# The input projections in another order, and all sixteen gates computed within dilated attention

## The chip, the cores and the metric

The kernel runs on one core of a Trainium2 chip. The metric is the device time of one execution in microseconds (us); less is better. TensorE multiplies matrices, VectorE (DVE), ScalarE (ACT) and GpSimd (POOL) work on the elements, and transfers are issued from the queues of SyncE (SP) and of ScalarE.

## The reference

One decoder layer for 1024 tokens of width 1024, in float32. One input projection gives eight parts; two head groups read them, each group has a SiLU gate, and the result goes through an output projection, a residual and a layer norm:

```python
h = x @ w_in
c_q, c_kv, k_rope, g_a, q_b, k_b, v_b, g_b = jnp.split(h, offs, axis=-1)
y_a = mla_attention(c_q, c_kv, k_rope, ...) * jax.nn.silu(g_a)   # 8 heads, causal
y_b = dilated_attention(q_b, k_b, v_b) * jax.nn.silu(g_b)        # 8 heads, dilations 1, 4, 16
x = layernorm(DEEPNORM_ALPHA * x + jnp.concatenate([y_a, y_b], -1) @ w_out, ln_g, ln_b)
```

The latents c_q (384 columns) and c_kv (256) pass an RMS norm and an up-projection before the latent attention; the dilated queries and keys are rotated.

## The kernel before

Every float32 operand of a projection is split into a high and a low part, and each product is made of three matmuls (`PASSES`: high by high, high by low, low by high) that accumulate in one bank of PSUM. The high part is an ACT copy, the low part a subtraction on DVE, or on POOL for weights (`hi_lo`, L77; `wload`, L110). The 1024 rows of the contraction are eight tiles, `KD`; the tokens are two halves `s` of 512 or eight blocks `i` of 128.

The projections follow each other in this order: the first four tiles of the latents while x arrives, with the contraction outermost and all eight banks in use (L127 to L153); the up-projections' weights are loaded, scaled and stored as float16 pairs beside them (`u_load`, `u_scales`, `u_split`, L208 to L212); the fifth latent tile (L269); the dilated values, block by block (`v_block`), with the latents' normalisation between them (`rms_apply`, L243); half of the latent attention's values (`va_block`, L347); the dilated queries (`qk_block(0, ...)`); the other half of the latent values; the keys (`qk_block(1, ...)`); and then eight of the sixteen gates, which are those of the first half of the tokens (`gate_now`, L451, called in L455 and L507).

Queries, keys and values are brought to float16 pairs by a power of two. The largest value over all partitions takes a way through DRAM and back (`pow2`, L289): a DVE reduction, a store, a load that spreads it, and another DVE reduction that waits for that load. Only then do `q_split`, `k_split` and `v_split` write the pairs to DRAM (`q_d`, `k_d`, `v_d`), from which `load_qk` (L478) brings them back by transposing transfers, two for the queries and two for the keys of each pair of heads.

Dilated attention has 32 steps (four pairs of heads, two halves, four blocks). A step is scores (`dil_scores`, TensorE), the mask and the row's least value (L551, DVE), the exponential (`dil_expo`, ACT), the split of the probabilities (`dil_high`, `dil_low`), a transposing transfer for every two steps (`ptd`), and the product with the values five steps later (`dil_values`). The mask is loaded whole (`mraw`, L498) and brought to the scores' units by two DVE instructions (L501, L502). Between the steps `next(fill, None)` emits a piece of other work for TensorE: half a gate (12 matmuls), and after the last gate a piece of what the latent attention needs first (`latents_first`, L678). The list `FILL` (L800) names the steps that have one piece; the eight gates of the second half of the tokens are 16 such pieces, and step 22 has the last of them. Those gates use Tanh from the table that Exp is in, and one DVE instruction more than the eight before, which use Silu; each weight of a gate is loaded twice in the program, once for each half of the tokens.

The memory of a phase lies where that of an earlier one was: `gy`, `b4` (nine slots of 4 KB), `b8` and the mask `mp` of dilated attention take the place of the projections' weights (`wp`) and working tiles (`st`), and a tile waits for what lay in its place. x lies on the other side, its first half so that it can be given up early (`stX0`). Each engine executes its instructions in the order in which a planner put them: it goes by the order of the program, and by the times that it reckons with where an instruction isn't ready.

The latent attention and the output projection follow. The second key tile of the latent attention (`kB`, L845) lies in `b8`; beside the last pair of heads the first weights and gated rows of the output projection are prepared in the memory of the latents (`open_pools(stO, side="right")`, L910; `load_wo`, `load_y`).

Of the kernel before, what the change touches and what calls it, by code (L numbers as in the profile page):

```python
# [19 lines left out]
P = 128  # L20
# [20 lines left out]
def tile_hybrid_layer(ctx, tc, xT, xres, w_c, w_c2, w_vr, w_k, w_q, w_g, w_u, w_o,  # L41
# [53 lines left out]
    stG, stX0, st1, stPS1 = (ctx.enter_context(ExitStack()) for _ in range(4))  # L95
# [5 lines left out]
    wp, st = l1("wp", 10), l1("st")  # L101
# [8 lines left out]
    def wload(src, n, name, pool=None):  # L110
        r = rtile(name + "r")
# [5 lines left out]
    xs = [[xp[s].tile([P, 2, 512], F32R, name=f"x{k}{s}") for s in range(2)] for k in range(KD)]  # L117
    acc = [bank(f"acc{m}") for m in range(8)]
# [3 lines left out]
    SMALL = {2: ((qg_s, qg), (kvg_s, kvg)), 4: ((csd, cs_dil), (csp, cs_pe), (mmla, msk_mla))}  # L122
    heat = st.tile([P, 512], F16, name="heat")
    nc.vector.memset(heat, 0.0)
    for _ in range(HEAT):
        nc.tensor.matmul(acc[7], heat[:, :P], heat, start=True, stop=True)
    for k in range(KD):  # L127
        if k in SMALL:  # what is needed later only does not hold the first rows up
            for d, src in SMALL[k]:
                tc.keep_in_program_order(nc.scalar.dma_start(d, src))  # L130
        xr = [rtile(f"xr{k}{s}")[:, :512] for s in range(2)]
        if k == 0:  # the first product waits for little
            r = rtile("wc0r")
            ws = wp.tile([P, 2, 544], F32R, name="wc0", tag="w")
            for c in (slice(0, P), slice(P, 512)):
                sync.dma_start(r[:, c], w_c[0, :, c])
                nc.scalar.copy(ws[:, 0, c], r[:, c])
                if c.start == 0:
                    sync.dma_start(xr[0], xT[:P, half(0)])
                    nc.vector.tensor_copy(xs[0][0][:, 0], xr[0])  # L140
                    nc.vector.tensor_sub(xs[0][0][:, 1], xr[0], xs[0][0][:, 0].bitcast(F32))
# [6 lines left out]
        order = [(s, m, pz) for s in range(2) for m in range(4) for pz in PASSES]  # L148
        if k == 0:
            order = [(s, m, pz) for s in range(2) for pz in PASSES for m in range(4)]  # L150
# [60 lines left out]
    for a in uraw:  # L211
        u_split(*a)  # L212
# [912 lines left out]
```

## Time and profile before

| | us |
|---|---|
| median of three runs | 660.19 |
| lowest and highest run | 656.34, 662.71 |
| the profiled execution, its span from the first to the last instruction | 659.7 |
| TensorE busy in that span | 601.3 |
| VectorE busy | 417.7 |
| ScalarE busy | 327.5 |
| GpSimd busy | 317.8 |

No time other than its span is given for the profiled execution. Busy TensorE includes matmuls that overlap in the pipeline, so that a stretch in which it is always busy can still hold fewer or more matmuls; the number of matmuls in a stretch tells how fast it went.

### The profile page before, as it was taken

What the parts mean: (1) busy time and instruction counts of PE and PEld (TensorE: products, weight loads), DVE (VectorE), ACT (ScalarE), POOL (GpSimd) and SP (SyncE); (2) the same over time, 40 slices, a digit from 0 to 9 for tenths busy, and PEclk for the clock granted to TensorE, in tenths of its full rate; (3) what the DMA queues carried; (4) which work ended last, traced back from release to release, by engine and by line L of the source; (5) the groups of instructions that cost most, each with busy time, mean ns of one, the idle gap of its engine ahead of it and who ended that gap; (6) DMA issues with size and microseconds to landing.
All of it is one profiled execution on the core that took longest, in us unless ns stands there. A gap on an engine that the chain in (4) does not pass through costs nothing.

```text
span 659.7 us, 11049 instructions
## 1 busy us (share of the span) xinstructions
PE 601.3 (91%) x3975; PEld 439.9 (67%) x3975; DVE 417.7 (63%) x865; ACT 327.5 (50%) x661; POOL 317.8 (48%) x338
## 2 busy tenths in 40 slices
PE   8999999999999979399999987889789878799995
PEld 5777999788688858166666644545445445678884
DVE  5671299443234042357876798598699998454886
ACT  3467323334423254168675785488588876440000
POOL 2148323925814265267774576374357595640000
PEclk9999999999999979689999978898799997999998
DMA  8695112876812469999999799939869999861051
GB/s 287 203 285 171 33 33 80 116 226 158 222 43 94 36 240 177 182 219 230 230 209 195 160 302 201 199 58 195 154 116 181 156 224 242 200 202 67 1 192 64
DMA packets 200854, 108.53 MB, mean 165 GB/s; under 512 B 158688, under 2 KB 176608, under 8 KB 200672
## 3 DMA queue, kind: packets, MB, share of 16 engines
q1 hardware_dynamic: 194608, 96.36, 63.5%
q10 hardware_dynamic: 6192, 11.47, 7.7%
q8 instruction: 31, 0.51, 0.4%
q14 instruction: 23, 0.19, 0.1%
HBM read 48.30 MB, written 20.71 MB: 105 GB/s over the span
## 4 chain that ended last, share of the span: by engine, by line
PE 36%; DMA 28%; DVE 15%; POOL 6%; issue 6%; ACT 5%; SPq 3%; ACTq 0%; DVEq 0%; POOLq 0%
PE op L880 8%; DMA pT<-ph 6%; DMA ptd<-p 5%; PE gP L429 5%; DMA kk<-k_d 3%; PE op L1009 3%; DMA xr<-in_xT_dram 3%; PE Od L623 3%; PE vbA L223 3%; PE vbB L223 3%; PE qg L700 2%; DVE p L745 2%; PE Sd L544 2%; PE Sd L547 2%; DVE ph L777 2%
## 5 line engine op out<-in xcount | busy, mean ns | idle before, releaser
L429 PE MATMUL gP<-x,wg 128*128 128x512 f32 x384 | 96.5, 408 | 3.5 <-ACT wg L78 2.9
L429 PEld LDWEIGHTS gP<-x,wg 128*128 128x128 f32 x384 | 73.7, 196 | 21.3 <-ACT wg L78 3.3
L880 PE MATMUL op<-wo,ys 128*128 128x512 f32 x288 | 68.4, 394 | 0.0
L880 PEld LDWEIGHTS op<-wo,ys 128*128 128x128 f32 x288 | 54.0, 189 | 11.9 <-issue 0.4
L750 ACT ACTIVATE p<-p,sm 128x128 f32<-128x128 f32 (+3 forms) x64 | 49.1, 767 | 11.1 <-DVE sm L745 9.9
L745 DVE CUSTOM_DVE_ANT_0 p<-S,mask,fs 128x128 f32<-128x128 f32 (+3 forms) x64 | 50.4, 808 | 2.8 <-PE S L739 1.4
L557 ACT ACTIVATE td<-td,st 128x384 f32<-128x384 f32 (+1 forms) x64 | 42.3, 661 | 18.2 <-DVE st L551 18.1
L551 DVE CUSTOM_DVE_ANT_0 td<-Sd,mdil,dsc 128x384 f32<-128x384 f32 (+1 forms) x64 | 41.5, 680 | 14.0 <-PE Sd L547 12.8
L152 PE MATMUL acc<-x,wc 128*128 128x512 f32 x192 | 46.9, 405 | 1.8 <-DVE x L140 1.3
L544 PE MATMUL Sd<-kk,qq 64*128 64x256 f16 (+1 forms) x128 | 37.2, 291 | 12.1 <-DMA kk<-k_d 11.1
L789 PE MATMUL O<-pT,v 128*64 128x256 f16 (+1 forms) x480 | 31.8, 274 | 16.2 <-DMA pT<-ph 14.5
L739 PEld LDWEIGHTS <-q 128*128 128x128 f16 x288 | 25.6, 99 | 30.5 <-issue 9.3
L152 PEld LDWEIGHTS acc<-x,wc 128*128 128x128 f32 x192 | 36.9, 194 | 12.2 <-issue 2.2
L223 PE MATMUL qkP<-wk,x 128*128 128x512 f32 x192 | 44.7, 394 | 0.0
L223 PE MATMUL qkP<-wq,x 128*128 128x512 f32 x192 | 44.3, 392 | 0.0
L775 POOL TENSOR_TENSOR ph<-p,ph 128x256 f16<-128x256 f32 (+3 forms) x32 | 36.7, 1155 | 14.4 <-ACT ph L768 14.3
L766 POOL TENSOR_SCALAR p<-p,sm 128x256 f32<-128x256 f32 (+3 forms) x32 | 28.5, 897 | 31.3 <-DVE sm L756 15.1
L777 DVE SCALAR_TENSOR_TENSOR ph<-p,sm,ph 128x128 f16<-128x128 f32 (+3 forms) x32 | 37.3, 1177 | 8.1 <-ACT ph L768 8.0
L590 POOL TENSOR_TENSOR p<-td,p 128x384 f16<-128x384 f32 (+1 forms) x32 | 37.0, 1162 | 10.3 <-ACT p L580 10.0
L223 PEld LDWEIGHTS qkP<-wk,x 128*128 128x128 f32 x192 | 36.1, 188 | 8.4
L223 PEld LDWEIGHTS qkP<-wq,x 128*128 128x128 f32 x192 | 36.0, 188 | 8.1
L789 PEld LDWEIGHTS <-v 128*64 128x64 f16 x480 | 27.5, 114 | 19.5 <-issue 14.3
(324 smaller groups left out, 1236.7 us busy)
## 6 DMA issues: line engine op xcount, KB each, us to landing
xr<-in_xT_dram SPq DMA_DIRECT2D x16, 256.0 KB, 4.2
v_d<-v SPq DMA_DIRECT2D x16, 256.0 KB, 3.1
wor<-in_w_o_dram SPq DMA_DIRECT2D x8, 512.0 KB, 4.3
xr<-in_xres_dram SPq DMA_DIRECT2D x16, 256.0 KB, 3.1
out_dram<-xr SPq DMA_DIRECT2D x16, 256.0 KB, 2.0
k_d<-k SPq DMA_DIRECT2D x8, 384.0 KB, 2.7
u<-in_w_u_dram SPq DMA_DIRECT2D x10, 256.0 KB, 5.2
c_d<-c SPq DMA_DIRECT2D x10, 256.0 KB, 2.5
```

Source lines behind the costliest of these rows:

```text
L152: nc.tensor.matmul(acc[m * 2 + s], ws[:, a, m * P:(m + 1) * P], xs[k][s][:, b], **flags(k, KD, (a, b)))
L223: nc.tensor.matmul(dst, xs[k][i // 4][:, a, (i % 4) * P:(i % 4) * P + P], w8[k][:, b, o:o + w], **flags(k, KD, (a, b)))
L429: nc.tensor.matmul(p, wg[k // 4][:, a, (k % 4) * P:(k % 4) * P + P], xs[k][s][:, b], **flags(k, KD, (a, b)))
L544: nc.tensor.matmul(S[e][:, (ns - 2) * P:], q[:, i * P:i * P + P], rhs, start=(w == 0), stop=False)
L551: nc.vector.tensor_tensor_reduce(TD[u_][:, e, :ns * P], S[e], mk, dsc[:, 1:2], BIG, ALU.add, ALU.min, stt[:, e, 0:1])
L557: nc.scalar.activation(t[:, :w], t[:, :w], AF.Exp, bias=ST[u_][:, e, 0:1], scale=-1.0, accum_out=ST[u_][:, e, 1:2])
L590: nc.gpsimd.tensor_sub(p16[:, e, 1], t, p16[:, e, 0])
L745: nc.vector.tensor_tensor_reduce(t[:, :w], S[:, :w], M["mask"][:, T - w:], fs[:, 7:8], BIG, ALU.add, ALU.min, sm[:, 0:1])
L750: nc.scalar.activation(TT[u][:, :w], TT[u][:, :w], AF.Exp, bias=SM[u][:, 0:1], scale=-1.0, accum_out=SM[u][:, 1:2])
L777: nc.vector.scalar_tensor_tensor(p16[:, :, 1], t, SM[u][:, 3:4], p16[:, :, 0], ALU.mult, ALU.subtract)
L789: nc.tensor.matmul(O[ME[e], q0:], V[hp][:, kb, vh, ME[e]], rhs, **flags(kb, 2 * ch + 2, (vh, phl)))
L880: nc.tensor.matmul(op[i][:, half(c)], ys[k][a][:, i * P:(i + 1) * P], ws[k][b][:, half(c)], **flags(n_, KD, (a, b)))
```

## The change

The queries are projected first, while x arrives, then keys, values and last the latents. Each of these runs with the contraction outside and two to eight blocks inside. The queries' and keys' splits and the up-projections' weights move beside the values; the latents' normalisation and all eight blocks of latent values come at the end. No gate is computed before dilated attention: all sixteen are pieces between its first 24 steps, one a step and a second one in every third, with Tanh in place, the two halves of the tokens one after the other for the same weights, which are loaded once. x stays whole until then. Working tiles grow from 18 to 24, `b4` shrinks from nine to eight, gate weights from four to three with two raw tiles of their own; the latents' second key tile lies beside the first; and the output projection has three instead of two of its gated rows prepared beside the last pair. The scratch for dynamic transfers is set to 1024 bytes. The core of the diff:

```diff
-    gwp, raw = rG("gwp", 4), rG("raw", 4)
-    xp = [None, rG("xp1")]
-    xp[0] = open_pools(stX0, side="right")("xp0")
+    gwp, graw, xp = rG("gwp", 3), rG("graw", 2), rG("xp")
...
-            ws = wload(w_c[k], 512, f"wc{k}")
+            ws = wload(w_q[k], 512, f"wq{k}")
...
+        for i, (a, b) in order:
+            nc.tensor.matmul(acc[i], xs[k][i // 4][:, a, (i % 4) * P:(i % 4) * P + P], ws[:, b, :512],
...
-    FB, CB = 18, 3
-    u_load()
-    u_scales()
-    for a in uraw:
-        u_split(*a)
+    FB, CB = 24, 3
...
+    wk_ = [wload(w_k[k], 512, f"wk{k}") for k in range(KD)]
+    for i in range(NB):
+        qk_out(0, i, acc[i])
+    for g in (range(4), range(4, NB)):
+        qk_blocks(1, wk_, g)
+    u_load()
+    pow2(qkm[:, 0], 2, "q", SC_DIL)
+    u_scales()
+    wvr = [wload(w_vr[k], 544, f"wvr{k}") for k in range(KD)]
+    for g in range(4):
+        v_blocks((2 * g, 2 * g + 1))
+        for i in (2 * g, 2 * g + 1):
+            q_split(qkf[0, i], i)
+            u_split(*uraw[i])
+        if g == 0:
+            pow2(qkm[:, 1], 3, "k", 1.0)
+        else:
+            for i in range(3 * g - 3, min(3 * g, NB)):
+                k_split(qkf[1, i], i)
...
+    c_blocks(((0, 0), (1, 0), (0, 1), (1, 1)))
+    for i in range(NB):
+        v_split(vfb[i], i)
+    pow2(krm, 4, "kr", 2.0 ** 14)
+    mla_scales()
+    rms_apply(0, 0)
+    rms_apply(0, 1)
+    c_blocks(((2, 0), (3, 0), (2, 1), (3, 1)))
+    c_blocks(((4, 0), (4, 1)))
+    rms_apply(1, 0)
+    rms_apply(1, 1)
+    for i in range(NB):
+        va_block(i)
...
-        if now:
-            nc.scalar.activation(g, p, AF.Silu)
...
+        g = GT[m, s] = gy.tile([P, 512], F32, name=f"g{m}{s}", tag="g")
+        nc.scalar.activation(g, p, AF.Tanh, scale=0.5)
+        nc.vector.scalar_tensor_tensor(g, g, 1.0, p, ALU.add, ALU.mult)
...
-    GATES = [(m, s) for s in range(2) for m in (4, 5, 6, 7, 0, 1, 2, 3)]
-    NPRE = 8
+    GATES = [(m, s) for m in (4, 5, 6, 7, 0, 1, 2, 3) for s in range(2)]
...
-    b4, b8, mp = left("b4", 9), left("b8", 2), left("mp")
+    b4, b8, mp = left("b4", 8), left("b8", 2), left("mp")
...
+    for _ in load_qk(0):
+        pass
+    load_v(0)
+    for _ in load_qk(1):
+        pass
...
+        K[1] = [lat.tile([P, 2, T], F16, name=f"kB{e}") for e in range(2)]
...
-            if n in FILL:
+            for _ in range(1 + (n % 3 == 0 and n < 24)):
                 next(fill, None)
...
-    kB = b8.tile([P, 2, 2, T], F16, name="kB", tag="kk")
-    K[1] = [kB[:, e] for e in range(2)]
...
-    NW, NWS, NYS = 2, 4, 4  # weights beside the last pair; the others follow
-    LOADW, LOADY, PROJ0, NY = (3, 8), (5, 8), (13, 15), 2
+    NW, NWS, NYS = 2, 4, 3
+    LOADW, LOADY, PROJ0, NY = (3, 8), (5, 8, 10), (13, 15), 3
...
-    nc = bacc.Bacc("TRN2", target_bir_lowering=False, num_devices=1)
+    nc = bacc.Bacc("TRN2", target_bir_lowering=False, num_devices=1, dynamic_dma_scratch_size=1024)
```

## Rows read from the trace of the kernel before

**Rows 1.** The page, busy time of an engine over the whole span.

```profile
PE 601.3 (91%) x3975; PEld 439.9 (67%) x3975; DVE 417.7 (63%) x865; ACT 327.5 (50%) x661; POOL 317.8 (48%) x338
```

**Rows 2.** Windows: busy time and instructions by engine, granted clock, share of transfers.

```profile
5.80:53.00 47.20, 46.67 (x192) 37.07 (x193) 33.36 (x61) 24.10 (x43) 16.16 (x12) 1.00 0.81 261
53.00:65.70 12.70, 11.60 (x51) 9.17 (x50) 0.69 (x1) 9.23 (x17) 11.76 (x10) 1.00 0.58 172
65.70:117.10 51.40, 51.40 (x393) 49.42 (x392) 37.28 (x49) 16.10 (x30) 17.01 (x15) 1.00 0.15 47
117.10:231.00 113.90, 113.90 (x501) 89.29 (x500) 37.15 (x85) 38.58 (x69) 55.02 (x90) 1.00 0.56 130
231.00:265.90 34.90, 31.38 (x126) 24.66 (x124) 12.27 (x24) 16.12 (x33) 20.87 (x19) 0.90 0.82 199
265.90:277.00 11.10, 0.02 (x1) 0.10 (x1) 5.13 (x2) 1.24 (x2) 2.53 (x2) 0.61 1.07 165
277.00:283.00 6.00, 5.94 (x44) 2.85 (x44) 2.88 (x11) 4.25 (x10) 2.58 (x2) 0.50 1.14 334
283.00:376.60 93.60, 93.39 (x902) 62.22 (x900) 66.68 (x167) 64.23 (x150) 60.12 (x64) 0.99 1.01 203
376.60:413.70 37.10, 31.83 (x365) 18.32 (x361) 33.09 (x74) 26.26 (x61) 25.77 (x33) 0.86 1.16 250
```

**Rows 3.** Windows in equal slices, one within the eight gates ahead of dilated attention.

```profile
247.50:264.00 16.50, 16.50 (x75) 13.65 (x74) 4.10 (x4) 6.50 (x13) 9.33 (x8) 1.00 1.01 176
```

**Rows 4.** Timeline around the first of those gates: start, duration, engine, idle before.

```profile
231.79 0.29 DVE L297 TENSOR_REDUCE km<-kmb 128x1 f32<-128x128 f32 x1 [12.71 <-DMA kmb<-k_d]
...
232.88 0.51 ACT L306 ACTIVATE k<-qn,scl 128x256 f16<-128x256 f32 x1 [9.42 <-DVE scl L302]
...
235.14 1.22 PE L429 MATMUL gP<-x,wg 128*128 128x512 f32 x2 [2.90 <-ACT wg L78]
```

**Rows 5.** Timeline of the changeover to dilated attention.

```profile
253.34 0.33 ACTq L498 DMA_DIRECT2D mraw<-in_msk_dil_dram  x1
...
254.61 15.89 SPq L484 DMA_TRANSPOSE kk<-k_d  x1
...
271.84 1.49 DVE L501 TENSOR_SCALAR mdil<-mraw 128x2560 f32<-128x2560 f32 x1 [19.41 <-DMA mraw<-in_msk_dil_dram]
...
273.36 3.82 DVE L502 SCALAR_TENSOR_TENSOR mdil<-mraw,dsc,mdil 128x2560 f32<-128x2560 f32 x1
...
277.06 0.37 PE L544 MATMUL Sd<-kk,qq 128*128 128x256 f16 x1 [11.14 <-DMA kk<-k_d]
...
281.44 4.88 PE L429 MATMUL gP<-x,wg 128*128 128x512 f32 x12
```

**Rows 6.** Timeline of TensorE alone, two steps of dilated attention.

```profile
317.16 3.02 PE L429 MATMUL gP<-x,wg 128*128 128x512 f32 x12
320.02 0.28 PE L544 MATMUL Sd<-kk,qq 128*128 128x256 f16 x1
...
321.55 3.02 PE L429 MATMUL gP<-x,wg 128*128 128x512 f32 x12
```

**Rows 7.** Timeline of DVE alone, normalisation of the query latent's two halves.

```profile
98.63 0.68 DVE L249 TENSOR_SCALAR rmv<-rbc 128x512 f32<-128x512 f32 x1
...
107.24 2.08 DVE L257 SCALAR_TENSOR_TENSOR craw<-craw,qg_s,rmr 128x512 f32<-128x512 f32 x3
...
115.55 5.02 DVE L257 SCALAR_TENSOR_TENSOR craw<-craw,qg_s,rmr 128x512 f32<-128x512 f32 x3
```

**Rows 8.** Windows in equal slices around those two halves' ends, columns as in Rows 2.

```profile
99.00:115.50 16.50, 16.50 (x130) 16.02 (x129) 15.48 (x19) 5.10 (x10) 5.05 (x5) 1.00 0.24 80
115.50:132.00 16.50, 16.50 (x81) 11.92 (x80) 7.40 (x10) 6.36 (x12) 16.50 (x15) 1.00 0.83 116
```

**Rows 9.** The line that transposes the dilated keys: issue to landing.

```profile
DMA to landing us min/median/max: 4.1/5.6/22.4
```

**Rows 10.** The output projection's weight tiles: low parts of the first two.

```profile
L86 POOL TENSOR_TENSOR wo<-wor,wo x2: 2367/2510/2653, 535.3 to 542.2; 128x1024 fp32r<-128x1024 f32 x2
```

More of the change, by code (lines that the diff above doesn't have):

```diff
@@ L110, in wload @@
     def wload(src, n, name, pool=None):
-        r = rtile(name + "r")
+        r = graw.tile([P, 512], F32, name=name + "r", tag="raw") if pool else rtile(name + "r")
         (nc.scalar if pool else sync).dma_start(r[:, :n], src)
@@ L132, in tile_hybrid_layer @@
         if k == 0:
[L133 to L141, printed above, removed]
+            r = rtile("wq0r")
+            ws = wp.tile([P, 2, 544], F32R, name="wq0", tag="w")
+            sync.dma_start(r[:, :512], w_q[0])
+            nc.scalar.copy(ws[:, 0, :512], r[:, :512])
+            nc.scalar.dma_start(xr[0], xT[:P, half(0)])
+            nc.vector.tensor_copy(xs[0][0][:, 0], xr[0])
+            nc.vector.tensor_sub(xs[0][0][:, 1], xr[0], xs[0][0][:, 0].bitcast(F32))
             nc.gpsimd.tensor_sub(ws[:, 1, :512], r[:, :512], ws[:, 0, :512].bitcast(F32))
         else:
-            ws = wload(w_c[k], 512, f"wc{k}")
+            ws = wload(w_q[k], 512, f"wq{k}")
         for s in range(k == 0, 2):
@@ L361, in tile_hybrid_layer, with qk_blocks, qk_out @@
     qkm = small.tile([P, 2, NB], F32, name="qkm", tag="qkm", bufs=1)
-    def qk_block(j, ww, i):
-        p = bank(f"qkP{j}{i}")
-        nat(p, ww, 0, 512, i)
+    def qk_blocks(j, ww, g):
+        banks = [bank(f"qkP{j}{i}") for i in g]
+        nat([(i, (p,)) for i, p in zip(g, banks)], ww, ((0, 512),))
+        for i, p in zip(g, banks):
+            qk_out(j, i, p)
+    def qk_out(j, i, p):
         n_ = qkf[j, i] = f_tile(f"qn{j}{i}")
@@ L432, in gate @@
                 yield
-        if first:
-            g = f_tile("g_first")
-        else:
-            g = GT[m, s] = gy.tile([P, 512], F32, name=f"g{m}{s}", tag="g")
-        if now:
-            nc.scalar.activation(g, p, AF.Silu)
-            if first:
-                nc.scalar.dma_start(g_d, g)
-        else:
-            d = four(f"gd{m}{s}", [P, 512], F32)
-            nc.scalar.activation(d, p, AF.Tanh, scale=0.5)
-            nc.vector.scalar_tensor_tensor(g, d, 1.0, p, ALU.add, ALU.mult)
+        g = GT[m, s] = gy.tile([P, 512], F32, name=f"g{m}{s}", tag="g")
+        nc.scalar.activation(g, p, AF.Tanh, scale=0.5)
+        nc.vector.scalar_tensor_tensor(g, g, 1.0, p, ALU.add, ALU.mult)
         yield
-    GATES = [(m, s) for s in range(2) for m in (4, 5, 6, 7, 0, 1, 2, 3)]
-    NPRE = 8
+    GATES = [(m, s) for m in (4, 5, 6, 7, 0, 1, 2, 3) for s in range(2)]
     GT, WG = {}, [None, None]
-    def gate_now(m, s, bank_, first=False):
-        for _ in gate(m, s, bank_, True, first):
-            pass
-    gate_now(*GATES[0], bank, True)
-    nc.vector.tensor_scalar(scl[:, 0:2, 2:3], scl[:, 0:2, 1:2], 0.5, None, ALU.mult)
-    q_split(qkf[0, NB - 1], NB - 1)
-    pow2(qkm[:, 1], 3, "k", 1.0)
-    for i in range(NB):
-        k_split(qkf[1, i], i)
     st1.close()
```

130 lines of the change are left out of this document (46 added, 84 removed).

## The prediction

> **What bounds the kernel now.** I read the page first: TensorE is busy 601.3 of the span's 659.7 us, the next engine 417.7 [rows 1]. So the time is TensorE's, and the question is where it doesn't run, or runs slowly. The windows tell, by the number of matmuls rather than by the busy time [rows 2]. The yardstick is a stretch of nothing but gates: 75 matmuls of 512 columns in 16.5 us, 0.22 us each [rows 3]; a gate of 24 is 5.28 us. Against it:
>
> - The latents' products, which open the kernel, take 47.20 + 12.70 = 59.9 us for 192 + 48 matmuls, worth 52.8: 7.1 us lost [rows 2]. Ten loads and splits of up-projection weights run beside them.
> - Values, queries and keys run close to that pace: 501 matmuls in 113.9 us, 0.227 each [rows 2].
> - The gates ahead of dilated attention take 34.9 us for 126 matmuls, worth 27.7: 7.2 us lost [rows 2]. The cause is in the timeline: DVE waits 12.71 us for the keys' largest value to come back from DRAM, ACT waits 9.42 us for DVE, and the copy of a gate's weights is queued behind that on ACT, so that TensorE waits too [rows 4].
> - At the changeover TensorE has one instruction in 11.1 us, at a granted clock that falls to 0.61 on average [rows 2]; the next 6 us are at 0.50, the lower level, 1.2 GHz. What it waits for are the keys' transposing transfers, issued at 254.61 and used at 277.06; the mask came at the same time, loaded from 253.34 to 271.84 and ready 5.3 us later [rows 5].
> - From there to 376.6 TensorE is busy 93.4 of 93.6 us while DVE, ACT and POOL have 60 to 67 [rows 2]. It is the bound of the steps that have pieces of gates. This decides about the change: a gate that is moved into those steps isn't hidden there, it lengthens them.
> - From 376.6 to 413.7, where the gates are used up, TensorE idles 5.3 us and DVE has 33.1 of 37.1 [rows 2].
>
> **The change part by part**, against the span of 659.7 (0.5 below the median of 660.19).
>
> *The first product, and what is beside it.* The same 192 matmuls of the same shape come first, now for the queries. The up-projections' loads, reductions, splits and stores leave this stretch, and the fifth latent tile with its wait on an eviction leaves too. Of the 7.1 us lost I give back 3. Ends: all 7, and minus 1 for a first product that waits for a weight tile of 512 instead of 128 columns. **-3.**
>
> *The round trip of the keys' scale.* It lies beside the values now, where 48 us of products are queued. Eight banks cover one late eviction, since a group of two value blocks takes four. But four more round trips stand in the same row on DVE and ACT: a wait such as the 12.71 us [rows 4] blocks every eviction and weight copy behind it. A group is 96 matmuls, about 12.5 us at the pace of the values now, 393 in 51.4 us [rows 2]; so one such wait is just covered, two in a row aren't. I take back 6 of the 7.2; ends: all 7.2, and 6 more lost instead. **-6.**
>
> *Eight gates moved.* Ahead of dilated attention half a gate costs 2.64 us. Within it the next scores start 2.86 us after it: 317.16 to 320.02 [rows 6]. 16 halves x 0.22 = 3.5. Ends 0 (where two halves follow each other) and 6. The extra DVE instruction for each of the eight, and one split of each weight less on ACT and POOL, lie beside TensorE, which has 93.4 of 93.6; they count nothing unless DVE becomes the bound, at 66.7 us for 22 steps some 3 us a step against 4.4 (317.16 to 321.55 [rows 6]). **+3.5.**
>
> *The changeover.* What goes is 11.1 us, and what the low clock took after it: two steps' scores in 4.38 us (277.06 to 281.44 [rows 5]) instead of 2 x 1.53 (320.02 to 321.55 [rows 6]), and half a gate of 4.88 instead of 3.02: together 14.3. **-14.3.** What comes in its place is the greatest unknown. The last latent products are followed by a chain of their own, the query latent's normalisation, two halves on DVE, 98.63 to 120.57 in the trace, 21.9 us [rows 7]. Key tiles, mask and much else of dilated attention lie where its working tiles were (by the code some 13 of 24 are in use at the end), so I expect that neither is issued before that chain ends. Then the transfers take 5.6 us at their median, 22.4 at their worst [rows 9], the mask 18.5 as it did, and 5.3 for its preparation [rows 5]. With the median transfer that is 21.9 + 5.6 + 5.3 = 33 us from the last latent product to the first masked score; with the mask's load as measured 46. TensorE has 48 matmuls of latent values for it, 10.6 us at 0.22. There remain 22 to 35, the middle 29, and only gates can cover them: they depend on x, on weights with memory of their own, on two banks, and on one DVE instruction each that frees a bank. DVE is the engine that normalises, so two gates for certain, and about two more once it is free: 21 us. Left over are 8, and 3.2 for a clock that falls as it did: **+11**. Ends: 2 where all is covered, 28 where it is two gates and the mask as late as now (35 - 10.6 + 3.2). A gate brought forward costs nothing later: even with six, 20 of the 32 halves remain for the first 24 steps, and now there are 16.
>
> Here a rule speaks against the change. The third part of each half's normalisation, of the same shape, took 2.08 us in one half and 5.02 in the other [rows 7]; POOL was busy 5.05 and 16.5 of 16.5 us around them [rows 8]. The Trainium skill (GPSIMD Engine Reference, Key points) says that POOL shares its SBUF interfaces with DVE, and that DVE instructions with two SBUF inputs contend for them. The trace agrees: 2.08 against 5.02. By that rule the chain is at its longer length in its new place, since POOL splits gate weights there; without it, it would be some 19 us and the sum 3 lower.
>
> *The end.* The latents' second key tile moves into the memory that the output projection's first tiles take beside the last pair of heads, so one weight tile or two of the gated rows must wait for the last scores. POOL has 2.5 us for such a low part [rows 10]; TensorE has other products to do there in part. Ends 0 and 5. **+1.5.**
>
> Sum: 659.7 - 3 - 6 + 3.5 - 14.3 + 11 + 1.5 = **652.4**.
>
> **The rivals.**
>
> *The gates cover the changeover whole*: six are brought forward and TensorE never waits: 2 instead of 11 gives 643. For it: gates are ready from the end of the latents on, and the planner moves what is ready (half a gate stands right behind two steps' scores [rows 5], where the program has it behind the third's). Against it: in the trace nothing was moved ahead of the first scores, and TensorE stood for 11.14 us; I read this as a landing that the planner reckoned with earlier, and that may come again.
>
> *The changeover grows*: slower. The normalisation on DVE holds back the instruction that frees a gate's bank, two gates are done, and TensorE stands until keys and mask have come. At 28 us, two gates and the mask as late as now, the time is 669; with the middle's 29 - 10.6 + 3.2 = 22 it is 663. It decides against the change from 19 on, where the sum reaches 660. For it: the chain of 22 us is new in that place, the mask's load can't start before it, and the gates' DVE instructions may be queued behind the one that waits for the mask. Against it: DVE has gaps in the chain, where it waits for ACT's root.
>
> *The round trips only move*: what the keys' scale cost ahead of the gates comes back beside the values, +6 instead of -6: 664, within 1%.
>
> *The moved gates are hidden after all*, if the steps aren't TensorE's: 3.5 and 16 x 2.64 less, 607. The busy rows speak against it; I give it almost nothing.
>
> **How the numbers follow.** Three runs span 1%, so about 1% is what can be told from no change: 653.5 and 666.8 are the bounds. Forecast (647 to 658) 0.44, covered whole (638 to 647) 0.20, changeover grows (662 to 674) 0.20, round trips move (658 to 667) 0.11, hidden or something else 0.05. Faster by over 1%: 0.24 of the forecast, which its middle just reaches, all of the second and the last, 0.49. Slower: 0.17 of the third and 0.04 of the fourth. The range leaves out the edges of second and third: 637 to 670.
>
> **What would show it.** In the windows after: queries' 192 matmuls in less than 47 us after the first; no wait of TensorE of over 2 us until the latents end, which should be at about 215 us (265.9 - 42.2 for eight gates - 3 - 6); then gates ahead of the first scores, four of them, and an idle stretch of under 10 us with keys or mask as its releaser; steps of 4.4 us with one half and 7.0 with two (4.4 + 2.64); no change from step 24 on. Wrong would be: fewer than three gates ahead of the first scores, a first step later than 255 us, weight copies on ACT queued behind `q_split` or `k_split`, or an output projection that starts with waits for its first weights.

## The result

The changed kernel takes 706.44 us (median of four runs, 705.96 to 707.05) against 661.06 (656.34 to 662.71) for the kernel before: a ratio of 1.0693, interval 1.0636 to 1.0751. The prediction of 652.4 was wrong in its sign. The profiled executions are 704.5 and 659.7 us long, 44.8 apart. Beside the experiments the kernel before ranged more widely (650.76 to 671.73 at the most), and the ratios given there go by its executions within 1.5% of its fastest.

The page after answers to [rows 1]: TensorE has 9 us more of busy time, and the span is 45 us longer.

```profile
PE 610.7 (87%) x3975; PEld 441.3 (63%) x3975; DVE 421.6 (60%) x873; ACT 318.9 (45%) x643; POOL 298.2 (42%) x322
```

The windows after, cut where the work changes (columns as in [rows 2]): queries, keys, values, the first group of latents, a gap, the other latents, the latent values, the changeover, the steps with gates, the rest of dilated attention, and what follows the last latent scores.

```profile
6.56:54.87 48.31, 47.58 (x193) 37.45 (x194) 16.70 (x21) 23.80 (x39) 27.75 (x29) 1.00 0.68 208
54.87:99.25 44.38, 44.38 (x194) 36.08 (x192) 11.48 (x26) 11.76 (x25) 23.50 (x47) 1.00 0.21 62
99.25:151.80 52.55, 49.61 (x385) 49.39 (x384) 34.49 (x89) 20.03 (x45) 15.68 (x25) 0.97 0.49 170
151.80:174.20 22.40, 22.37 (x98) 17.98 (x96) 9.02 (x18) 5.87 (x13) 13.50 (x14) 1.00 0.33 104
174.20:201.70 27.50, 0.04 (x1) 0.04 (x1) 8.81 (x28) 7.46 (x12) 1.31 (x1) 0.54 0.43 122
201.70:246.90 45.20, 42.32 (x152) 30.66 (x153) 19.91 (x20) 12.12 (x20) 11.81 (x9) 0.88 0.15 44
246.90:257.90 11.00, 11.00 (x50) 5.10 (x49) 10.78 (x10) 2.80 (x5) 0.00 (x0) 0.96 0.13 48
257.90:284.40 26.50, 12.58 (x49) 9.68 (x48) 14.48 (x17) 9.29 (x15) 11.26 (x8) 0.83 0.83 214
284.40:415.90 131.50, 131.45 (x1069) 90.49 (x1068) 71.41 (x184) 70.04 (x161) 60.18 (x64) 0.97 0.80 166
415.90:465.50 49.60, 42.20 (x493) 23.39 (x493) 40.58 (x89) 32.09 (x70) 28.06 (x36) 0.93 0.93 216
592.00:704.50 112.50, 97.76 (x492) 78.51 (x492) 72.31 (x140) 21.76 (x44) 34.13 (x22) 0.93 0.50 140
```

One line stands out: from 174.2 to 201.7 no engine is busy for even 9 of 27.5 us. The timeline tells who waits for whom there (start, duration, engine, line; in brackets the idle time before and its releaser):

```profile
201.66 2.08 PE L242 MATMUL rbc<-sq,ones 128*128 128x512 f32 x2 [27.49 <-POOL sq L231]
...
173.34 0.29 DVE L287 TENSOR_REDUCE vbm<-vbmb 128x1 f32<-128x128 f32 x1 [12.60 <-DMA vbmb<-vb_d]
...
186.91 0.28 DVE L287 TENSOR_REDUCE krm<-krmb 128x1 f32<-128x128 f32 x1 [10.07 <-DMA krmb<-kr_d]
...
194.51 0.75 DVE L297 SCALAR_TENSOR_TENSOR v<-vb,scl,v 128x512 f16<-128x512 f32 x1 [2.90 <-ACT v L296]
...
197.71 1.28 DVE L226 COPY craw<-cP 128x512 f32<-128x512 f32 x2
...
188.35 0.72 ACT L296 ACTIVATE v<-vb,scl 128x512 f16<-128x512 f32 x1 [12.34 <-DMA vb_d<-v]
...
160.77 0.33 SPq L284 DMA_DIRECT2D vb_d<-vbm  x1
168.46 0.32 SPq L286 DMA_DIRECT2D vbmb<-vb_d  x1
```

TensorE waits for the sum of squares on POOL, but POOL has been idle, too. The first group's products are complete at 174.2, and their copies out of PSUM (`craw`) start only at 197.71. What stands ahead of them on DVE are the round trip of the values' scale (12.60), that of the rotary key's (10.07) and the splits of the values, of which each waits for ACT, and ACT for the five stores of a split two back. So the releaser in the PE row is the last link, and the cause is three links back. The two trips stand one behind the other: the second one's store is issued at 174.36, though the rotary key's numbers were ready at 165.4, because its reduction stood on DVE behind the wait for the first.

The keys' own round trip, which the prediction was about, lies beside the values and costs little there: DVE waits 10.70 us for it, and TensorE 2.94, for a bank.

```profile
124.80 0.28 DVE L287 TENSOR_REDUCE km<-kmb 128x1 f32<-128x128 f32 x1 [10.70 <-DMA kmb<-k_d]
...
127.01 0.64 PE L121 MATMUL vbA<-wvr,x 128*128 128x272 f32 x3 [2.94 <-ACT vb L273]
```

The changeover after, to set beside [rows 5]:

```profile
272.31 7.09 PE L443 MATMUL gP<-x,wg 128*128 128x512 f32 x24 [8.92 <-DVE v L331]
284.45 0.37 PE L532 MATMUL Sd<-kk,qq 128*128 128x256 f16 x1 [5.05 <-DMA kk<-k_d]
...
270.93 0.60 ACT L330 ACTIVATE v<-vaP 128x512 f16<-128x512 f32 x1 [3.40 <-DMA v_d<-v]
...
271.56 0.69 DVE L331 SCALAR_TENSOR_TENSOR v<-vaP,v 128x512 f16<-128x512 f32 x1 [3.73 <-ACT v L330]
280.47 1.49 DVE L496 TENSOR_SCALAR mdil<-mraw 128x2560 f32<-128x2560 f32 x1 [8.22 <-DMA mraw<-in_msk_dil_dram]
281.88 0.68 DVE L450 SCALAR_TENSOR_TENSOR g<-g,gP 128x512 f32<-128x512 f32 x1
```

To compare the stages, I leave the gates out: a gate is 5.28 us wherever it stands, by the prediction's yardstick. With all 192 matmuls of eight gates ahead of its first scores, the kernel before has its projections done at 265.9 - 42.2 = 223.7; the changed one at 257.9 (its two gates come later). So +34.2. Then to the first scores: 26.55 - 10.56 = 16.0 against 11.1, +4.9. From the first scores to the end of the last product of dilated attention (465.55; 425.39 before): 181.1 with 14 gates against 148.3 with eight, 32.8 where six gates are 31.7, +1.1. From there to the end: 239.0 against 234.3, +4.7. Together 44.9, of 44.8.

### The profile page after: what moved, and what is told of

Its sections match the earlier page's. It is cut to its first block, busy times and chain, and to the rows that moved or that the text cites. A ratio compares the mean times of both kernels' runs of the same rounds, so it can differ in the third digit from the quotient of the medians.

```text
span 704.5 us, 10974 instructions
## 1 busy us (share of the span) xinstructions
PE 610.7 (87%) x3975; PEld 441.3 (63%) x3975; DVE 421.6 (60%) x873; ACT 318.9 (45%) x643; POOL 298.2 (42%) x322
## 4 chain that ended last, share of the span: by engine, by line
PE 48%; DMA 16%; DVE 16%; POOL 7%; issue 6%; ACT 4%; SPq 1%; DVEq 0%; ACTq 0%; POOLq 0%
PE gP L443 12%; PE op L866 9%; PE acc L158 6%; PE cP L220 5%; PE Sd L532 3%; PE op L995 3%; PE Sd L535 3%; DMA pT<-ph 3%; DVE p L734 3%; DVE ph L766 3%; PE Od L611 2%; PE O L778 1%; DMA kk<-k_d 1%; PE S L728 1%; POOL wvr L79 1%
## 5 line engine op out<-in xcount | busy, mean ns | idle before, releaser
L866 PE MATMUL op<-wo,ys 128*128 128x512 f32 x288 | 71.0, 402 | 5.9 <-POOL wo L86 3.7
L866 PEld LDWEIGHTS op<-wo,ys 128*128 128x128 f32 x288 | 54.9, 193 | 18.7 <-POOL wo L86 4.2
L220 PE MATMUL cP<-x,wc 128*128 128x512 f32 x240 | 58.5, 407 | 0.0
L220 PEld LDWEIGHTS cP<-x,wc 128*128 128x128 f32 x240 | 46.8, 195 | 11.5 <-ACT rmr L245 0.5
L539 DVE CUSTOM_DVE_ANT_0 td<-Sd,mdil,dsc 128x384 f32<-128x384 f32 (+1 forms) x64 | 41.6, 680 | 18.6 <-PE Sd L535 14.6
L158 PE MATMUL acc<-wq,x 128*128 128x512 f32 x192 | 47.7, 409 | 2.8 <-ACT x L78 2.1
L766 DVE SCALAR_TENSOR_TENSOR ph<-p,sm,ph 128x128 f16<-128x128 f32 (+3 forms) x32 | 40.1, 1269 | 11.9 <-ACT ph L757 11.9
L563 POOL TENSOR_SCALAR td<-td,st 128x384 f32<-128x384 f32 (+1 forms) x32 | 21.6, 680 | 59.1 <-DVE st L551 48.4
L158 PEld LDWEIGHTS acc<-wq,x 128*128 128x128 f32 x192 | 37.3, 195 | 13.7 <-ACT x L78 3.0
L778 PE MATMUL O<-pT,v 128*64 128x256 f16 (+1 forms) x480 | 33.5, 282 | 9.0 <-DMA pT<-ph 7.5
L755 POOL TENSOR_SCALAR p<-p,sm 128x256 f32<-128x256 f32 (+3 forms) x32 | 26.8, 849 | 32.6 <-DVE sm L745 18.9
```

Of the source, the lines that this page charges most:

```text
L158: nc.tensor.matmul(acc[i], xs[k][i // 4][:, a, (i % 4) * P:(i % 4) * P + P], ws[:, b, :512], start=(k == 0 and (a, b) == (0, 0)), stop=(k ...
L220: nc.tensor.matmul(dst, ww(k, a, m), xs[k][s][:, b], **flags(k, KD, (a, b)))
L539: nc.vector.tensor_tensor_reduce(TD[u_][:, e, :ns * P], S[e], mk, dsc[:, 1:2], BIG, ALU.add, ALU.min, stt[:, e, 0:1])
L766: nc.vector.scalar_tensor_tensor(p16[:, :, 1], t, SM[u][:, 3:4], p16[:, :, 0], ALU.mult, ALU.subtract)
L778: nc.tensor.matmul(O[ME[e], q0:], V[hp][:, kb, vh, ME[e]], rhs, **flags(kb, 2 * ch + 2, (vh, phl)))
L866: nc.tensor.matmul(op[i][:, half(c)], ys[k][a][:, i * P:(i + 1) * P], ws[k][b][:, half(c)], **flags(n_, KD, (a, b)))
```

## The experiments

In all of them the mark "values' end" is the end of the last latent value product, "gates" the number of gate matmuls ahead of the first dilated scores, and "rest" the time from the last dilated product to the end. All are read from the one profiled execution of each, in us; that of e17 is the slowest of its four, 6 us above their median.

| new order | values' end | gates | first scores | last dilated product | rest | span |
|---|---|---|---|---|---|---|
| after | 257.9 | 48 | 284.5 | 465.6 | 239.0 | 704.5 |
| e1_next_products_first | 238.7 | 53 | 264.0 | 447.8 | 240.2 | 688.0 |
| e2_round_trips_later | 256.2 | 48 | 283.1 | 463.8 | 240.1 | 703.9 |
| e3_second_key_tile | 255.5 | 48 | 282.5 | 463.3 | 237.3 | 700.6 |
| e5_no_round_trips | 237.3 | 48 | 263.4 | 445.1 | 239.8 | 684.8 |
| e6_after_first_group | 240.0 | 48 | 265.2 | 449.2 | 239.7 | 688.9 |
| e7_after_all_groups | 230.0 | 165 | 293.4 | 458.0 | 239.7 | 697.7 |
| e11_later_no_round_trips | 230.1 | 48 | 257.3 | 439.3 | 239.0 | 678.3 |
| e12_all_mended | 227.5 | 48 | 253.8 | 435.6 | 242.4 | 678.0 |
| e17_changed_nine_slots | 255.2 | 48 | 281.4 | 469.8 | 244.0 | 713.8 |

| order of before | gates | first scores | last dilated product | rest | span |
|---|---|---|---|---|---|
| before | 192 | 277.1 | 425.4 | 234.3 | 659.7 |
| e4_gates_alone | 174 | 269.1 | 430.5 | 238.1 | 668.6 |
| e8_gates_alone_old_end | 174 | 266.7 | 428.8 | 240.5 | 669.3 |
| e9_before_eight_slots | 192 | 270.7 | 432.0 | 241.4 | 673.4 |
| e10_gates_alone_nine_slots | 172 | 267.7 | 424.7 | 242.7 | 667.4 |
| e13_before_small_scratch | 192 | 277.4 | 422.3 | 233.4 | 655.7 |
| e14_before_own_key_tile | 192 | 269.5 | 415.0 | 240.5 | 655.5 |
| e15_before_changed_end | 192 | 272.1 | 418.9 | 235.2 | 654.1 |
| e16_nine_slots_gates_ahead | 192 | 272.5 | 415.4 | 241.5 | 656.9 |
| e18_best_of_parts | 192 | 272.6 | 417.4 | 238.2 | 655.6 |

### The stall: e1, e2, e5, e6, e7, e11

**e1** takes TensorE's sums out of the way: the product with ones that starts the normalisation stands behind the next groups.

```diff
     c_blocks(((0, 0), (1, 0), (0, 1), (1, 1)))
...
-    rms_apply(0, 0)
-    rms_apply(0, 1)
     c_blocks(((2, 0), (3, 0), (2, 1), (3, 1)))
     c_blocks(((4, 0), (4, 1)))
+    rms_apply(0, 0)
+    rms_apply(0, 1)
     rms_apply(1, 0)
```

> The changed kernel, with the two normalisations of the key/value latent put behind all latent products instead of behind the first group. DVE still has its two round trips and ACT its eight value splits ahead of the latents' evictions. Theory, blocked evictions: the 27.5 us in which TensorE stands come from DVE and ACT being held up, and from the sums that TensorE has ahead of its next products; with 96 products of the next group put first, 21 of these us are covered and the clock stays up. Stall under 8 us, time 674 to 684 against 706. Rival, the chain decides: the normalisation is needed anyway before anything later can start, so that first scores come no earlier than 280 us and the time stays at 700 to 707. Rival, the sum on POOL, which the wait names, is late for a reason of its own: the same stall, behind the second group.

688.86 us, ratio 1.0503 [1.0431, 1.0574]: 17.6 less than the changed kernel, and 16.2 less than e2 below, which ran beside it. That is between the ranges of the theory and its rival. The 192 products of the first two groups run through without a wait; DVE still waits 12.24 and 10.20 us for the two scales, and part of the time comes back as a wait of the latent values for the normalisation:

```profile
153.89 44.54 PE L220 MATMUL cP<-x,wc 128*128 128x512 f32 x192
199.42 11.38 PE L220 MATMUL cP<-x,wc 128*128 128x512 f32 x48 [0.99 <-DVE craw L226]
...
225.15 7.52 PE L326 MATMUL vaP<-uv,c 128*128 128x512 f16 x24 [9.85 <-ACT c L257]
```

So the stall needs both: a late sum, and products that stand behind it on TensorE though they don't need it.

**e2** moves the values' splits, the rotary key's round trip and its scales behind the third group in the program's text (the five lines from `for i in range(NB): v_split(...)` to `mla_scales()`), and nothing else.

> The changed kernel, with the eight value splits, the round trip of the rotary key's scale and the scales of the latent attention moved from behind the first group of latent products to behind the third. Theory, blocked evictions: DVE copies the first group out at once (174 to 177 us), the sums come at about 178, TensorE's stall of 27.5 us shrinks to under 6, the end of the latents moves from 258 to about 225 us; the moved splits take DVE time ahead of dilated attention, so the time is 676 to 688. Rival, POOL: the stall stays. Rival, the changeover takes it back: latents end by 30 us earlier, first scores by less than 10, time 697 to 707.

705.1, ratio 1.075 [1.068, 1.082]: no change. DVE waits 12.54 us at 174.30 and 9.80 at 187.60, and TensorE 28.82, as in the changed kernel. The planner put these instructions in the same order on the engines although the text had them elsewhere. So this run doesn't test the theory; the next ones set the order by data.

```profile
202.49 2.08 PE L242 MATMUL rbc<-sq,ones 128*128 128x512 f32 x2 [28.82 <-POOL sq L231]
```

**e5** leaves the two trips through DRAM out; the scales come from each partition's own largest value, raised to 4, which for this input gives the same numbers; other inputs would need the trips.

```diff
-        d = dpool.tile([P, 1], F32, name=nm + "_d")
-        sync.dma_start(d, m1)
+        if j in (2, 3):
+            d = dpool.tile([P, 1], F32, name=nm + "_d")
+            sync.dma_start(d, m1)
...
-        pow2_of(e, m1, 2.0 ** -40)
+        pow2_of(e, m1, 2.0 ** -40 if j in (2, 3) else 4.0)
```

> The changed kernel, but the scales of the values and of the rotary key take each partition's own largest value (raised to at least 4, which for this input gives the same power of two), so that their two ways through DRAM and back are left out; their local reductions, the splits and the stores stay. Theory A (in-order blocking): in the changed kernel DVE waits 12.60 and 10.07 us for the two loads, with the latents' evictions queued behind them, and TensorE's stall of 27.49 us ends with these. Without them the stall is 5 to 10 us (the splits' own 8 x 2 instructions are left) and the time is 680 to 690. Theory B (the splits' pace): the eight splits of the values share two tiles and wait for five stores each; then the stall stays above 20 us and the time within 5 of 706.

**e6** and **e7** keep the trips and let them depend on a late latent tile, of the first group (e6, as shown; the first group's normalisation then stands ahead of them) or the last (e7, by `craw[4, 1]`; there they also stand behind the latent values):

```diff
+    for mx in (vmb[:, 0:1], krm):
+        nc.vector.scalar_tensor_tensor(mx, craw[1, 1][:, 0:1], 0.0, mx, ALU.mult, ALU.max)
+    pow2(vmb, 1, "vb", 1.0 / PSC)
     for i in range(NB):
         v_split(vfb[i], i)
```

> The changed kernel, but the largest values of the values and of the rotary key pass one more small instruction that also reads the last latent tile of the first group, so that both round trips and the splits of the values can only start behind that group's evictions, and stand behind the key/value latent's normalisation in the program. Theory A: the stall of 27.49 us shrinks to under 5, the latents end 20 to 25 us earlier than the 257.9 of the changed kernel, and the time is 680 to 690. Theory B or a wait that only moves: the same waits now stand ahead of the next groups' evictions or of the query latent's normalisation, TensorE stands as long there, and the time stays at 700 to 710.

> As the run before it, but the round trips and the splits of the values wait for the last of the ten latent tiles and stand behind the latent values in the program. Theory A: no stall above 5 us until the latent values end, at 225 to 232 instead of 257.9; if the dilated values come in time for step 5, the time is 675 to 685. Rival: the values' own stores and loads now end so late that the first product with dilated values, or the gates in front, wait for them, and what was won is given back: 695 or more.

**e11** is e6 with e5's scales.

> The changed kernel with the scales of the values and of the rotary key from each partition's own largest value (raised to 4), thus without their ways through DRAM, and with the splits of the values behind the first latent group's evictions. Leaving out the round trips alone left a stall of 11.98 us behind the splits; moving both alone left 12.19 behind the round trips. Theory (two separate blocks, each worth about 12 to 15 us): neither stall is left, the latent values end at 230 to 236, and the time is 674 to 682. Rival (one of them takes the place of the other whatever the order): a stall of 8 us or more is left and the time is 684 or more.

e5: 684.08, ratio 1.0406 [1.0333, 1.0479]. e6: 689.62, 1.0492 [1.0404, 1.058]. e7: 699.68, 1.0669 [1.0567, 1.0772]. e11: 678.78, 1.0341 [1.0268, 1.0414]. TensorE's waits for the sums, timelines of e5, e6, e7 and e11 in this order:

```profile
184.78 4.29 PE L242 MATMUL rbc<-sq,ones 128*128 128x512 f32 x4 [11.98 <-POOL sq L231]
```

```profile
175.48 1.12 PE L242 MATMUL rbc<-sq,ones 128*128 128x512 f32 x2 [1.40 <-POOL sq L231]
...
225.96 3.72 PE L242 MATMUL rbc<-sq,ones 128*128 128x512 f32 x4 [12.19 <-POOL sq L231]
```

```profile
176.62 1.12 PE L242 MATMUL rbc<-sq,ones 128*128 128x512 f32 x2 [1.40 <-POOL sq L231]
...
217.13 1.12 PE L242 MATMUL rbc<-sq,ones 128*128 128x512 f32 x2 [2.21 <-POOL sq L231]
...
262.26 29.47 PE L445 MATMUL gP<-x,wg 128*128 128x512 f32 x117 [8.83 <-DVE g L452]
...
283.93 5.07 SPq L481 DMA_TRANSPOSE kk<-k_d  x1
```

```profile
176.69 1.12 PE L242 MATMUL rbc<-sq,ones 128*128 128x512 f32 x2 [1.40 <-POOL sq L231]
...
217.22 1.13 PE L242 MATMUL rbc<-sq,ones 128*128 128x512 f32 x2 [2.22 <-POOL sq L231]
```

Without the trips 11.98 us are left: five splits, 2.3 to 3 us apart, still stand ahead of the copies. With the trips behind the first group they block the next group's copies instead, 12.19. With both away neither stall is left, and the values end at 230.1 instead of 257.9. So the theory of in-order blocking holds, and the splits' pace, which I had as its rival, is true as well: each is worth some 12 to 15 us of the 27.5. e7's rival came true: its values end as early as e11's, but the eight splits and their stores now fill SP's queue from 259.78 on, the keys' transposes are issued at 283.93 instead of 274.84, and with 165 gate matmuls done ahead TensorE still waits; 6.8 of 28 us are kept.

### The end and the gates: e3, e4, e8, e9, e10, e12

**e3** gives the second key tile memory of its own in the changed kernel; **e4** is the changed kernel with its projections replaced by those of before, so that all gates and the end are as changed; **e8** is e4 with e3's key tile and the third gated row behind the last pair instead of beside it.

```diff
-        K[1] = [lat.tile([P, 2, T], F16, name=f"kB{e}") for e in range(2)]
+        kbp = rq("kbp")
+        K[1] = [kbp.tile([P, 2, T], F16, name=f"kB{e}") for e in range(2)]
...
-    LOADW, LOADY, PROJ0, NY = (3, 8), (5, 8, 10), (13, 15), 3
+    LOADW, LOADY, PROJ0, NY = (3, 8), (5, 8), (13, 15), 2
```

> The changed kernel, with the latents' second key tile in memory of its own instead of beside the first, so that the output projection's first weights don't lie over it. Theory, the tail: the first two weights' splits on POOL come ahead of the last scores again (they came at 592 and 600 us, after the last scores at 591.5), and the stretch from the last scores to the end shrinks from 112.5 to about 103 us as before the change: time 695 to 699. Rival: the 9 us come from the third gated row that is prepared beside the last pair, or from a low clock: 704 to 707.

> The projections in the order of the kernel before, with everything else as changed: x whole, all sixteen gates within dilated attention, the second key tile beside the first. Theory, moved gates cost little: TensorE's time is moved, not added; but the keys' scale and splits now come right before dilated attention with no gates that must precede it, so that the changeover grows by 10 to 20 us, and the tail's 9 us are here too: 675 to 690. Rival, the gates are the loss: dilated attention with sixteen gates costs the 45 us by itself, 700 or more. Rival, they are hidden: 650 to 662.

> The order of projections of the kernel before, all sixteen gates within dilated attention, and at the end two things put back: the latents' second key tile in memory of its own, not in that of the output projection's first weights, and the third gated row loaded behind the last pair and not beside it. Gates alone with the changed end took 669.56, whose stretch after the last scores was 8 us longer than before. Theory (the end is what the gates' version lost): 658 to 662, the same as before within 1%. Rival (the second key tile's earlier place costs beside the last pair what it saves behind it, as it did in the changed kernel): 666 to 670.

e3: 704.26, ratio 1.0749 [1.0693, 1.0805]; e4: 669.56, 1.0208 [1.014, 1.0277]; e8: 671.7, 1.0223 [1.017, 1.0276]. In e3 the stretch behind the last latent scores is 103.8 instead of 112.5 us, and the one before it 150.0 instead of 142.9: what the place gives back is spent earlier. e4 shows that the order of projections is the greater part, about 36 of 45 us between the profiled executions, and that gates and end cost 9 (14 by the ratio). It lies below the 675 to 690 of its theory; the changeover didn't grow: the first scores come at 269.1, with 18 matmuls fewer ahead, against 277.1. e8 doesn't take the 9 us back; it lies next to its rival's range.

**e9** is the kernel before with `left("b4", 8)`; **e10** is e8 with nine slots and two gate weight tiles (`rG("gwp", 2)`); **e12** is e11 with e10's end and slots.

> The kernel before with one thing changed: the pool b4, which holds dilated attention's tiles, then the latent attention's probabilities and values, and last four pairs of output-projection weights, has eight slots as in the changed kernel instead of nine. Theory (the missing slot is what the end lost, since eight weight tiles and probabilities that are still in use want more than eight slots): 665 to 671, the loss after the first latent scores. Rival (the second key tile's place or the third gated row did it): 658 to 663, no difference from before.

> The gates-alone kernel with the end put back as far as before (second key tile in memory of its own, two gated rows beside the last pair), and b4 with nine slots; the room comes from the gate weights, which have two tiles instead of three. It took 671.7 with eight slots, with 152.2 us from the first to the last latent scores where before has 142.9. Theory (the slot): that stretch comes back to 142 to 145 and the time to 659 to 664. Rival (another cause in the latent stretch): 669 to 673. A gate that waits for its weights, now that no tile is free for the next one, would show as waits of TensorE in the dilated steps.

> The run before this one in the list with the end of before as well: nine slots of b4 (two gate weight tiles), the second key tile in memory of its own, two gated rows beside the last pair. Theory (three causes that add up: round trips, splits' pace, slots): 8 to 10 us below the run without the slots, 665 to 673; what is left above before is the changeover, 5 to 10 us. If the sum holds, nothing in the new order of the products itself costs time. Rival: 676 or more, a cause that is not named yet.

e9: 675.8, 1.0304 [1.0253, 1.0355], 20 us by the ratio for one slot of 4 KB, more than I had expected; from the first dilated scores to the end it takes 402.7 us instead of 382.6. e10: 668.84, 1.0193 [1.0142, 1.0243]; e12: 683.41, 1.0419 [1.0347, 1.0491]. The rivals again: nine slots don't bring the time back, alone or with the stall mended.

### What of the end is open: e13 to e18

**e13** is before with `dynamic_dma_scratch_size=1024`; **e14** adds e8's places of key tile and rows; **e15** instead adds the changed kernel's end (`K[1]` in `lat`, three rows, `NYS = 3`); **e16** is e10 with `for g in GATES[:8]` in front of `load_qk(0)` and before's `FILL`.

> The kernel before with the scratch for dynamic transfers at 1024 bytes, nothing else. If the scratch slows transfers at the end, 666 to 670; if it only frees memory, as the program suggests, within 1% of before, 655 to 665.

> The kernel before with the small scratch, the latents' second key tile in memory of its own on the other side, and the first of the four later gated rows in a third tile beside the last pair instead of in b8. No gate is moved, nine slots. Theory (the end's order of tiles is what costs: the rows' and weights' tiles come free later): 665 to 670 with 103 + 4 us or more behind the last latent scores. Rival (the gates moved into dilated attention cost it): 657 to 663.

> The kernel before with the small scratch and the changed kernel's end alone: the second key tile beside the first, where the output projection's first tiles come, and three gated rows beside the last pair, three behind it. Nine slots, no gate moved. Theory (the place holds back the first weights until the last scores, 9 us): 666 to 671, the split of the first weights on GpSimd behind the last scores as in the changed kernel. Rival (that split is not what ends late, the gates or the slots are): 657 to 663.

> The gates-alone kernel with nine slots (668.84), but eight of the sixteen gates stand ahead of dilated attention in the program again and the steps have the pieces of the kernel before. Theory (the gates in dilated attention cost the end): 657 to 663. Rival (the end's own changes): 665 to 671, unchanged.

663.73, 662.9, 656.29 and 659.42 us, beside a median of 663.26 for the kernel before, which ran next to them from 650.76 to 671.73; no interval is given. So in none of the four is a cost of the scratch, the tiles' places or the changed end seen, and with that spread one of up to 2% isn't excluded. The places do show in a stage: e14 has a rest of 240.5, 7.1 us more than e13, which it had won at the changeover. And e16 is 9.4 below e10 (10.6 between the profiled executions), from which it differs in eight gates alone. Where: e10 has its first scores 4.8 us earlier with 20 matmuls fewer done, which is about even; then it takes 157.0 us to the last dilated product and e16 142.9, though 20 matmuls more are only 4.4, so that 9.7 are left. The windows of the steps with gates, e10's and then e16's:

```profile
267.65:377.40 109.75, 106.51 (x946) 70.66 (x945) 66.92 (x179) 64.94 (x154) 57.33 (x61) 0.94 1.00 189
```

```profile
272.50:365.70 93.20, 93.20 (x906) 62.04 (x905) 63.86 (x172) 61.64 (x147) 51.36 (x57) 1.00 1.01 202
```

e16's TensorE is never idle and at 1.00; e10's idles 3.2 us, for transposing transfers of the probabilities (`ptd`) and not for a gate's weights, and its clock is 0.94 in the mean, 0.06 x 109.75 = 6.6 us: together 9.8, about the 9.7.

**e17** is the changed kernel with nine slots and two gate weight tiles, **e18** e16 with the changed end.

> The changed kernel with b4 at nine slots instead of eight, the room taken from the gate weights (two tiles instead of three); nothing else. Theory (the slot sets the end's 9.4 us): from the first latent scores to the end 244 to 249 instead of 255.4, and 695 to 700 in all. Rival (the end is longer for another reason): 252 or more there and 703 to 708 in all.

> The order of projections of the kernel before, eight gates ahead of dilated attention, whole x, the changed end and nine slots: e16 with the second key tile and three gated rows as the changed kernel has them. If e15's end (244 us from the first latent scores on) and e16's start (first latent scores at 404.7) add up: 648 to 654, 1 to 2% faster than before. Rival (what is won ahead of the latent scores is lost behind them, as in e14 and e16): 656 to 662, no difference.

e17: 709.53, 1.0837 [1.0782, 1.0892], its rest 244.0: the slot isn't it. e18: 654.28, 1.0003 [0.9976, 1.0031]: the same, and no kernel here is shown to beat the one before.

## Why the prediction was wrong

**The round trip of the keys' scale (-6)** is the step that failed. With the first product (-3) it put the latents' end, gates left out, 9 us earlier; it came 34 later. The price of one trip was right: 12.60 and 10.07 us beside 12.71 [rows 4]. For the keys' own trip the step nearly held: beside the values it made TensorE wait 2.94 us, where 1.2 had been left for it. The step even named four more trips on DVE and ACT, said that one such wait is just covered and two in a row aren't, and then bounded the loss at 6; its rival "the round trips only move" was right in kind and far too small, at +6. It counted banks: eight, of which a group takes four. But in the 27.5 us nothing waited for a bank. Behind the first group TensorE had a product that needs the result of that group's copies, and 144 products that need nothing stood behind it; e1 moves that product and gets 16 to 18 us back. And the step worked out only where the keys' trip goes. In the kernel before, DVE waited 1.2 us for the values' trip and 0.3 for the rotary key's; in the new order two of them and eight splits came directly ahead of the latents' copies. e5, e6 and e11 show each part. The stall's cost is the 27.5 us and a clock of 0.88 in the 45 us behind it, 0.12 x 45.2 = 5.4 us more.

**The first product (-3)** was mis-sized: it took 48.31 us and not under 47.2, so that 6.1 us were lost on 192 matmuls worth 42.2, where 4.1 were forecast. The pace of 501 matmuls in 113.9 us was read as that of values, queries and keys; the values lie in the row before it, and 68 of the 501 are gates. No term hangs on that.

**The changeover (-14.3 + 11)**: -3.3 was forecast, +4.9 measured. Two gates came ahead of the first scores, as in the rival "changeover grows". The second one waited 8.92 us for `DVE v L331`, a copy of latent values that frees a bank; that waited for ACT, and ACT 3.40 us for a store of earlier latent values; the normalisation had ended on DVE at 266.6. What held the third back is what that rival names: its bank is freed by the first gate's DVE instruction (L450), which came at 281.88, behind the one that waits for the mask. From the last latent product (241.6) to the first masked score (286.20) it took 44.6 us, of a forecast of 33 to 46. In part that is luck: the mask took 9.5 us from its issue and not 18.5, but it was issued only at 270.95, where the chain of 22 us would have ended at 263.5. The clock was low afterwards as I had it. From the latent values' end to the first scores it is 15 to 17 us without the gates in e5, e11 and e12 too, where less or nothing stalled ahead of it, and 16.0 here; so it belongs to the order.

On the rule that I weighed there: without POOL at work two steps of the normalisation took 0.68 (L248) and 0.69 us (L250); with POOL busy, 1.05 and 1.53. The Trainium skill (GPSIMD Engine Reference, Key points) says that POOL shares its SBUF interfaces with VectorE, which contends where an instruction has two SBUF inputs; the trace agrees. Its size was 1 to 2 us here, not the forecast's 3. The third parts, 2.06 and 2.08, met POOL only in their last 0.6 us, and what POOL did there were the normalisation's own low parts (L258), not the splits of gate weights, of which the first came at 277.39.

**Eight gates moved (+3.5)**: +1.1 in the changed kernel, of which six lie in the steps; TensorE is busy for 131.45 of 131.50 us there. The mechanism was right: a half costs its own time. e10 shows what the forecast left out: 9.7 us more in steps in which TensorE waited for transfers and the clock was low for a time.

**The end (+1.5, up to 5)**: +4.7 behind the last dilated product. The first weight tiles are late as forecast: TensorE idles 5.9 us before its first output products (L866), the most of it for their low parts on POOL, where it idled 0.0 before. With the key tile elsewhere (e3) that is 1.6, and the latent scores take 7 us longer instead. Which edit makes the 4.7 stays open: the slot, the key tile's place, the rows and the scratch were each tried, and none alone accounts for it in the changed kernel. The ninth slot is worth 20 us in the kernel before and nothing in the changed one; I have no reason for that which a run shows.

What remains in e11 over before is 18.6: values' end +6.4, changeover +5.5, dilated attention +2.0, rest +4.7. Why the values still end 6.4 later than before, where 9 earlier were forecast, no run takes apart; e11's trace has a wait of 2.75 us at the keys' trip and four for the sums of squares, together 5.05, which the kernel before has not.

Fewer than three gates ahead of the first scores, first scores after 255 us and waits for the first weights, which the prediction had named as signs of being wrong, all came.

## What to carry to other kernels

When a stage is moved, list for each in-order engine what will stand directly behind it there, not only what covers the moved step: in the changed kernel DVE's wait of 12.7 us for the queries' scale cost TensorE nothing beside the keys' products, and the two later ones with their splits cost it 27.5, since its next input stood behind them. Count TensorE's queue as well as its banks: one small product that needs a fresh result blocks all products behind it. And an edit of a program's text tests nothing until the trace shows that the engines' order moved.

## What the hardware showed

- A round trip of 128 numbers through DRAM took 12.6 us: the store is issued at 160.77, the dependent load at 168.46, 7.7 later, and DVE has it 4.9 after that. The Trainium skill (DMA: Bandwidth & Descriptors, Anatomy of one DMA) gives about 2.0 us of fixed time for one transfer, on GpSimd's path; by that, as an estimate, two would be 4 us. What was measured here, on SP's path and with transfers at a share of 0.04 in that stretch, is three times that, and it decides.
- With tiles that are only used at the end in another place, the changeover came earlier. Between e13 and e14 no instruction ahead of the latent attention differs, yet in the one profiled execution of each the first scores come at 277.37 and 269.47: the transposes of the first keys held SP for 16.59 us in one and 6.04 in the other, and the mask was 13.6 us earlier. By the program the second key tile and a gated row set the size of the slots of `b8`, and without them what lies behind shifts; that this is the reason, and how a place would act on the transfers, is not shown. What was won there was mostly given back later.

The rows of e13, then those of e14:

```profile
255.47 16.59 SPq L484 DMA_TRANSPOSE kk<-k_d  x1
273.38 1.49 DVE L501 TENSOR_SCALAR mdil<-mraw 128x2560 f32<-128x2560 f32 x1 [20.08 <-DMA mraw<-in_msk_dil_dram]
```

```profile
255.00 6.04 SPq L484 DMA_TRANSPOSE kk<-k_d  x1
...
259.80 2.61 DVE L501 TENSOR_SCALAR mdil<-mraw 128x2560 f32<-128x2560 f32 x1 [7.13 <-DMA mraw<-in_msk_dil_dram]
```
